# Hybrid decoder trunk on one core: projection pieces paced over all heads, a reciprocal in quarters, weight splits in halves

## The chip, the cores and the metric

One core of a Trainium2 chip runs the kernel as one program. The metric is the device time of one execution in microseconds. Before the change three executions took 1368.0, 1368.33 and 1369.17 us; the median is 1368.33 us.

## What is computed

Two layers, 512 positions of width 1024, all in fp32:

```python
h = rms_norm(x, attn_pre_norm[l])
proj = h @ w_in[l]                       # 1024 x 2844: q, k, v of three head groups
o_fox = fox_attention(...)               # 4 heads, causal, with a forget gate
o_nsa = nsa_attention(...)               # 8 heads, 2 key groups; compressed + selected + window branches
o_dil = dilated_attention(...)           # 4 heads
x = x + rms_norm(concatenate([o_fox, o_nsa, o_dil]) @ w_out[l], attn_post_norm[l])
h = rms_norm(x, ffn_pre_norm[l])
x = x + rms_norm((silu(a) * b) @ w_down[l], ffn_post_norm[l])   # a, b = causal conv(h @ w_up[l])
```

The compressed branch of the nsa heads makes its keys and values by `gelu(win @ w1) @ w2` over 31 windows of 32 positions.

## The kernel before, in words

**Products in two parts.** A weight arrives by DMA as fp32 (`raw`); `part_weights` (L137) makes a high part `wh` on ScalarE (ACT, L146) and the rest `wl = raw - wh` on VectorE (DVE, L154) or GpSimd (POOL, L150). Activations are split likewise (`hh`, `hl`; `ph`, `pl`; `mix`). Each product is three matmuls: high x high, low x high, high x low. `getw` (L202) issues the load of a weight two places ahead in a fixed plan and its split one or two places ahead. `DCUTS` (L42) lists the weights whose split is made in two instructions per engine instead of one, cut along the second axis (k). The weights `wo2` (rows 4 to 7 of `w_out`, 128x1x1024) have only one k, and are made whole.

**Attention as a list of units.** A unit is one head branch and one block t of 128 queries; 4 fox heads x 4, then 8 nsa heads x 2 branches x 4, then 4 dilated heads x 4 make 96 units (L1079). In slot i of the loop at L1241 the stages of different units run with fixed lags: scores of unit i on TensorE (PE, tile `s`), mask and minimum on DVE (L1126), exponential on ACT (L1131) and reciprocal on DVE (L1139), normalizing on POOL (L1143), transposes on PE five slots later (L1156, tile `pt`, two banks), the split of the transposed block on ACT (`ph`, L1167) and DVE (`pl`, L1172), and products with the values seven slots later (tile `o`). PE's order is the program's order (`tc.manual_schedule`); the other engines' order is set by the scheduler.

**Pieces between the units.** The projections that later heads need, the gelu's hidden layer, and the first half of the output projection are cut into pieces of about 12 matmuls (generator `main_pieces`, L750): 8 x 8 pieces of `proj256`, 2 x 4 of `hidden`, 16 of `out_first` (`wo`), 88 in all. `step()` issues one piece. A budget decides how many pieces follow each slot: it grows by 1.4 a slot in the first 12 slots and by 0.8 after that (`RATE`, L1231); a unit that needs a tensor not yet made forces pieces at once (`until`). After the 88, `out_start` (L918) issues nothing before slot 95; its pieces are the products with `wo2`.

**The gelu chain.** `cmp_pieces` (L938) makes gelu, compressed keys and values and the compressed scores, one step per slot (`chain_step`). One of its steps holds two reciprocals of 128x128 on DVE (L952). `cmp_values` then adds the compressed result to a head pair.

After the loop come the rest of the output projection, the norms, and the feed-forward part, whose first weights are `("up", 0, 0..3)`.

Of the kernel before, what the change touches and what calls it, by code (L numbers as in the profile page):

```python
# [12 lines left out]
AF = mybir.ActivationFunctionType  # L13
# [23 lines left out]
PCUT = ((0, 2), (2, 4))  # L37
# [1 line left out]
TT = "pt"  # L39
CT = "acc"  # L40
FIRST = 5
DCUTS = ("w1", "wo")  # L42
EV = (1, 3, 1, 1)
ORDER = (0, 1, 2, 4, 3, 5, 6, 7, 8)
HA0 = (1, 3)
# [29 lines left out]
def tile_hybrid_block(  # L75
# [6 lines left out]
    nc = tc.nc  # L82
# [12 lines left out]
    def nm(p):  # L95
        uid[0] += 1
        return f"{p}_{uid[0]}"
# [4 lines left out]
    def bt(shape, dt=F32, name="b"):  # L102
        return big.tile(shape, dt, tag="b", name=nm(name))

    def rt(shape=(128, 512), dt=F32):
        return rowp.tile(list(shape), dt, tag="r", name=nm("r"))
# [4 lines left out]
    def f(ap):  # L111
        return ap.bitcast(F32)
# [18 lines left out]
    def load(srcs, nk, ncol, tagn=""):  # L131
        raw = wpool.tile([128, nk, ncol], F32, tag="raw", name=nm("raw" + tagn))
        for s, k0, o in srcs:
            nc.sync.dma_start(raw[:, k0:k0 + s.shape[1], o:o + s.shape[2]], s)
        return raw

    def part_weights(raw, nk, ncol, spare, tagn, pool, cut):  # L137
        DCUT = ((0, 2), (2, 4)) if cut else ((0, 4),)
        if spare:
            hi, lo = bt([128, nk, ncol], F32R, "wh"), bt([128, nk, ncol], F32R, "wl")  # L140
        else:
            hi = wpool.tile([128, nk, ncol], F32R, tag="wh", name=nm("wh" + tagn))
            lo = wpool.tile([128, nk, ncol], F32R, tag="wl", name=nm("wl" + tagn))
        for a, e in HCUT if pool else DCUT:
            ks = slice(nk * a // 4, nk * e // 4)
            nc.scalar.activation(hi[:, ks], raw[:, ks], AF.Copy)  # L146
        if pool:
            for a, e in PCUT:
                ks = slice(nk * a // 4, nk * e // 4)
                nc.gpsimd.tensor_sub(lo[:, ks], raw[:, ks], f(hi)[:, ks])  # L150
        else:
            for a, e in DCUT:
                ks = slice(nk * a // 4, nk * e // 4)
                nc.vector.tensor_sub(lo[:, ks], raw[:, ks], f(hi)[:, ks])  # L154
        return hi, lo

    plan, ready = [], {}
# [2 lines left out]
    def kview(w, l):  # L160
        return w[l].rearrange("(k p) c -> p k c", p=128)

    for l in range(DEPTH):
        wi, wo, wu, wd = (kview(w, l) for w in (w_in, w_out, w_up, w_down))
# [37 lines left out]
    def getw(*key, ahead=AHEAD, pre=None, peek=False):  # L202

        i = where[key]
        pre = ahead if pre is None else min(pre, ahead)
        tag = lambda k: "_".join(str(z) for z in k)
        for n in range(len(done)):
            upto = i + (ahead, pre)[n]
            while done[n] < len(plan) and done[n] <= upto:
                k, srcs, nk, ncol, spare = plan[done[n]]  # L210
                if n == 0:
                    ready[k] = load(srcs, nk, ncol, tag(k))
                else:
                    ready[k] = part_weights(ready[k], nk, ncol, spare, tag(k), k[1] in ONPOOL or k[1:4] in ONPOOL or k[0:3] in ONPOOL,
                                            k[1] in DCUTS)
                done[n] += 1
        return None if peek else ready.pop(key)

# [142 lines left out]
    load_x(0)  # L361
    load_x(1)
    getw(0, "fk", 0, ahead=0, pre=-1, peek=True)
    grow = rt((2 * DEPTH * KT, 128))
    for i, src in enumerate((attn_pre_norm, ffn_pre_norm)):
        nc.sync.dma_start(grow[DEPTH * KT * i:DEPTH * KT * (i + 1), :], src.rearrange("l (k p) -> (l k) p", p=128))
    getw(0, "fk", 0, ahead=1, pre=-1, peek=True)
    load_x(2)
    getw(0, "fk", 0, ahead=2, pre=-1, peek=True)
    load_x(3)  # L370
    wk = []
# [76 lines left out]
    for l in range(DEPTH):  # L448
# [208 lines left out]
        nc.vector.tensor_scalar(gates, gates, 1.0, None, op0=ALU.add)  # L657
        nc.vector.reciprocal(gates, gates)

        mix, sums = {}, {}  # L660
        OFIRST = (0, 1, 2, 3)

        def split_mix(k, eng, cs=slice(0, 512)):
            if k not in mix:
                if k != 7:
                    mix[k] = bt([128, 2, 512], F32R, "mix")
                else:
                    mix[k] = ptp.tile([128, 2, 512], F32R, tag="ph", name=nm("mix"))
            d = mix[k]
            nc.scalar.activation(d[:, 0, cs], sums[k][:, cs], AF.Copy)  # L670
            eng.tensor_sub(d[:, 1, cs], sums[k][:, cs], f(d[:, 0, cs]))

        def o_mms(o, s, ks, w, first, last):

            sl = slice(128 * s, 128 * s + 128)
            for i, k in enumerate(ks):
                hi, lo = w[2 * i][:, 0], w[2 * i + 1][:, 0]
                mm(o, mix[k][:, 0, sl], hi, first and i == 0, False)
                mm(o, mix[k][:, 0, sl], lo, False, False)
                mm(o, mix[k][:, 1, sl], hi, False, last and i == len(ks) - 1)  # L680
# [20 lines left out]
        slot = [0]  # L701
        pieces, chain = Pieces(), []
# [47 lines left out]
        def main_pieces():  # L750
# [87 lines left out]

            for k in OFIRST:
                while k not in mix:  # L840
# [4 lines left out]
            def out_first():  # L845
                for qd in range(4):
# [3 lines left out]
                    for s in range(NST):  # L850
                        o_mms(sl256(pp, s), s, OFIRST, w4, s % 2 == 0, s % 2 == 1)
                        pieces.later(1, lambda s=s, q=sl256(pp, s), qd=qd: nc.scalar.activation(
# [32 lines left out]
        def mid_load(s):  # L885
            xt = bt([128, DM], name="x")
            nc.sync.dma_start(xt, x[0, 128 * s:128 * s + 128, :] if l == 0 else xsv[128 * s:128 * s + 128, :])
            xs.append(xt)
            hs.append(bt([128, DM], name="h"))
# [48 lines left out]
        def cmp_pieces(xc, w2r):  # L938

            t1, t2 = rt((128, 256)), rt((128, 256))  # L940
# [7 lines left out]
            nc.scalar.activation(t2, t1, AF.Exp, scale=-2.0 * math.sqrt(2.0 / math.pi))  # L948
            yield
            nc.vector.tensor_scalar(t2, t2, 1.0, None, op0=ALU.add)  # L950
            for c in range(2):
                nc.vector.reciprocal(t2[:, 128 * c:128 * c + 128], t2[:, 128 * c:128 * c + 128])  # L952
            yield
            nc.gpsimd.tensor_mul(xc, xc, t2)
            yield
            yield
# [105 lines left out]
        def step():  # L1062
            pieces.n += 1
            ended = next(fill, "end") == "end"
            pieces.due(last=ended)
            if ended and not chain:
                live[0] = False

        def chain_step():
            for c in chain:  # L1070
                if next(c, "end") == "end":
                    chain.remove(c)
# [6 lines left out]
        units = []  # L1079
# [132 lines left out]
        def cmp_values(k):  # L1212

            p = ps("pt")
            gq, part = k // 2, slice(64 * (k % 2), 64 * (k % 2) + 64)
            pch, pcl = store["pc"]
            vh, vl = (vcm[part, gq, i].rearrange("p u d -> p (u d)") for i in range(2))
            mm(p, vh, pch[part, gq, :], True, False)
            mm(p, vh, pcl[part, gq, :], False, False)
            mm(p, vl, pch[part, gq, :], False, True)  # L1220
            nc.vector.tensor_add(sums[2 + k], sums[2 + k], p)
            split_mix(2 + k, nc.gpsimd)
# [5 lines left out]
                mm(p[:, sl], hi[:, k, :], HL(k)[:, sl], False, False)  # L1228
                mm(p[:, sl], lo[:, k, :], HH(k)[:, sl], False, last and k == KORDER[-1])

        RATE = [1.4] * 12 + [0.8] * 98  # L1231
        LM, LN, LT, LE, LV, LO = LAGS
        stages = ((0, st_scores), (LE, st_keep_hi), (LM, st_max), (LN, st_norm), (LE, st_keep_lo), (LM, st_exp),
                  (LV, st_values), (LT, st_turn), (LO, st_out))
# [1 line left out]
        budget = 0.0  # L1236
        with tc.manual_schedule(engines={mybir.EngineType.PE}):
            for i in range(FIRST):
                step()
            for i in range(len(units) + LO):  # L1240
                slot[0] = i  # L1241
                U = lambda lag: units[i - lag] if 0 <= i - lag < len(units) else None
                for lag, fn in stages:
                    if U(lag) is not None:
                        fn(U(lag))
                budget += RATE[i]
                while budget >= 1.0:
                    budget -= 1.0
                    if live[0] or pieces.late:
                        step()  # L1250
                chain_step()
                if store.get("pc") and whole and whole[0][1] <= i:
                    cmp_values(whole.pop(0)[0])
            while whole or live[0] or pieces.late:
                if whole and store.get("pc"):
                    cmp_values(whole.pop(0)[0])
                elif live[0] or pieces.late:
                    step()
                    chain_step()
            for s in range(2):  # L1260
                mid_load(s)
            ws = [getw(l, "up", 0, n, ahead=0) for n in range(2)]
# [160 lines left out]
```

## Time and profile before

| what | before |
|---|---|
| median of the runs shown | 1368.33 us |
| the profiled execution's own time | 1369.85 us |
| its span, first to last instruction | 1367.9 us |
| PE busy | 1338.0 us (98%) |
| DVE, ACT, POOL busy | 850.4, 728.2, 287.0 us |
| granted TensorE clock, mean | 0.998 |

A profile's times are from the span's start. Layer 0's attention loop starts at about 62 us and its last unit's scores at 290 us; the feed-forward matmuls run to about 680 us; layer 1 repeats the same from there. A matmul's end is modelled, so a row's duration is its passage through the array, and the pace is read from one start to the next: 0.12 us for 128x256, 0.23 us for 128x512.

### The profile page before, as it was taken

The page shows a single profiled execution, that of the slowest core. Times are in us where ns is not written, and L with a number is a line of the kernel's source. Part 1 is how long each engine was busy: PE and PEld are TensorE (multiplying, and loading weights), DVE is VectorE, ACT ScalarE, POOL GpSimd, SP SyncE. Part 2 cuts the span into 40 slices and gives each one's busy share as a digit, 9 for nine tenths or more (in the row PEclk, how much of TensorE's full clock was granted, in tenths as well). Part 3 has the DMA queues.
Part 4 walks back from the last instruction along what each step waited for, and adds up shares of the span by engine and source line. Part 5 has one row for each costly group of instructions (what it writes and reads, how often), then busy time and mean ns, then how long its engine had stood idle before and what let it go on. Part 6 is the DMA issues. An engine that isn't in the chain of part 4 may idle for free.

```text
span 1367.9 us, 21028 instructions
## 1 busy us (share of the span) xinstructions
PE 1338.0 (98%) x7855; PEld 1177.9 (86%) x7855; DVE 850.4 (62%) x1893; ACT 728.2 (53%) x1506; POOL 287.0 (21%) x343
## 2 busy tenths in 40 slices
PE   9999999999999999999999999999999999999997
PEld 8899998978888888888898999999798888888886
DVE  7677787677755555433464887777876555554334
ACT  6567767777533333333465677667774333333232
POOL 2364753341000000000004647634210000000000
PEclk9999999999999999999999999999999999999999
DMA  6323311131333333333333242111323333332231
GB/s 181 94 63 115 104 35 48 58 128 33 107 93 103 97 92 96 104 93 123 111 96 93 63 139 63 47 41 58 120 62 98 103 92 93 104 97 92 94 122 62
DMA packets 145517, 123.74 MB, mean 90 GB/s; under 512 B 8264, under 2 KB 135688, under 8 KB 145416
## 3 DMA queue, kind: packets, MB, share of 16 engines
q1 hardware_dynamic: 145416, 122.40, 29.5%
q8 instruction: 62, 1.02, 0.3%
q14 instruction: 39, 0.32, 0.1%
HBM read 118.19 MB, written 4.19 MB: 89 GB/s over the span
## 4 chain that ended last, share of the span: by engine, by line
PE 85%; DVE 7%; ACT 4%; POOL 2%; issue 2%; DMA 0%; SPq 0%; ACTq 0%; POOLq 0%; DVEq 0%
PE acc L115 39%; PE s L115 19%; PE pt L115 13%; PE o L115 10%; PE pt L1156 3%; POOL wt L795 1%; PE pt L737 1%; DVE hl L271 1%; DVE pl L1172 1%; DVE r L1126 1%; ACT r L1131 1%; DVE x L913 0%; ACT hh L270 0%; ACT h L310 0%; ACT ph L1167 0%
## 5 line engine op out<-in xcount | busy, mean ns | idle before, releaser
L154 DVE TENSOR_TENSOR wl_up<-raw_up,wh_up 128x1024 fp32r<-128x1024 f32 x78 | 95.6, 1225 | 170.8 <-ACT wh_up L146 170.8
L146 ACT ACTIVATE wh_up<-raw_up 128x1024 fp32r<-128x1024 f32 (+1 forms) x90 | 89.6, 1001 | 160.4 <-PE acc L115 68.1
L154 DVE TENSOR_TENSOR wl_wd<-raw_wd,wh_wd 128x1024 fp32r<-128x1024 f32 x42 | 51.5, 1225 | 133.7 <-ACT wh_wd L146 133.7
L146 ACT ACTIVATE wh_wd<-raw_wd 128x1024 fp32r<-128x1024 f32 x42 | 44.5, 1060 | 144.8 <-PE pt L115 135.5
L1143 POOL TENSOR_SCALAR r<-r,sm,gates 128x128 f32<-128x128 f32 (+3 forms) x128 | 86.4, 683 | 126.1 <-DVE sm L1139 82.3
L1131 ACT ACTIVATE r<-r,sm 128x128 f32<-128x128 f32 x192 | 106.7, 557 | 9.3 <-DVE sm L1126 8.4
L115 PE MATMUL acc<-hh,wl_up 128*128 128x512 f32 (+1 forms) x272 | 102.4, 376 | 0.0
L115 PE MATMUL acc<-hl,wh_up 128*128 128x512 f32 (+1 forms) x272 | 102.4, 376 | 0.0
L115 PE MATMUL acc<-hh,wh_up 128*128 128x512 f32 (+1 forms) x272 | 102.4, 376 | 0.0
L150 POOL TENSOR_TENSOR wl_kc<-raw_kc,wh_kc 128x512 fp32r<-128x512 f32 x8 | 11.8, 1490 | 417.6 <-ACT wh_kc L146 416.8
L115 PE MATMUL s<-k,q 128*128 128x512 f32 (+3 forms) x384 | 96.2, 337 | 0.6 <-DVE sm L1126 0.6
L1172 DVE TENSOR_TENSOR pl<-pt,ph 128x384 fp32r<-128x384 f32 x144 | 85.6, 596 | 17.3 <-ACT ph L1167 15.9
L1167 ACT ACTIVATE ph<-pt 128x384 fp32r<-128x384 f32 x144 | 75.4, 523 | 29.1 <-PE pt L1156 27.9
L1126 DVE CUSTOM_DVE_ANT_0 r<-s,cmask 128x128 f32<-128x128 f32 (+3 forms) x160 | 76.0, 482 | 20.6 <-PE s L115 16.2
L1156 PE MATMUL pt<-ident,r 128*128 128x128 f32 x480 | 77.5, 276 | 7.0 <-DVE pl L1172 5.5
L115 PE MATMUL acc<-wh_wd,gh 128*128 128x512 f32 x252 | 83.7, 389 | 0.0
L115 PE MATMUL s<-hh,wh_up 128*128 128x512 f32 (+1 forms) x224 | 80.4, 359 | 0.0
L115 PE MATMUL s<-hl,wh_up 128*128 128x512 f32 (+1 forms) x224 | 80.4, 359 | 0.0
L115 PE MATMUL s<-hh,wl_up 128*128 128x512 f32 (+1 forms) x224 | 80.4, 359 | 0.0
L1347 ACT ACTIVATE r<-r 128x512 f32<-128x512 f32 x44 | 27.8, 632 | 85.7 <-DVE r L1328 85.5
L1156 PEld LDWEIGHTS pt<-ident,r 128*128 128x128 f32 x480 | 55.4, 141 | 15.9 <-POOL r L1143 6.8
L115 PE MATMUL acc<-wh_wo,mix 128*128 128x256 f32 (+1 forms) x296 | 67.6, 305 | 0.0
(439 smaller groups left out, 4121.2 us busy)
## 6 DMA issues: line engine op xcount, KB each, us to landing
raw_up<-in_w_up_dram SPq DMA_DIRECT2D x88, 512.0 KB, 3.8
raw_wd<-in_w_down_dram SPq DMA_DIRECT2D x44, 512.0 KB, 3.4
raw_wo<-in_w_out_dram SPq DMA_DIRECT2D x16, 512.0 KB, 3.5
x<-in_x_dram SPq DMA_DIRECT2D x8, 512.0 KB, 5.9
raw_nq<-in_w_in_dram SPq DMA_DIRECT2D x8, 512.0 KB, 3.7
raw_w<-in_cmp_w_k_dram SPq DMA_DIRECT2D x8, 512.0 KB, 4.0
raw_w<-in_cmp_w_v_dram SPq DMA_DIRECT2D x8, 512.0 KB, 4.2
raw_fk<-in_w_in_dram SPq DMA_DIRECT2D x4, 512.0 KB, 5.9
```

The source lines that it names most:

```text
L115: nc.tensor.matmul(o, lhsT=lhsT, rhs=rhs, start=start, stop=stop, skip_group_check=True)
L146: nc.scalar.activation(hi[:, ks], raw[:, ks], AF.Copy)
L154: nc.vector.tensor_sub(lo[:, ks], raw[:, ks], f(hi)[:, ks])
L271: nc.vector.scalar_tensor_tensor(lo, src, gain[:, k:k + 1], f(hi), op0=ALU.mult, op1=ALU.subtract)
L737: nc.tensor.transpose(p[:, 128 * s:128 * s + 128], tl[s][:, 128 * j:128 * j + 128], ident)
L1126: nc.vector.tensor_tensor_reduce(row[:, 0:n], u["S"][:, 0:n], u["mask"][:, 512 - n:512], op0=ALU.add, op1=ALU.min, scale=1.0, scalar=3.0e3 ...
L1131: nc.scalar.activation(row[:, 0:n], row[:, 0:n], AF.Exp, scale=-1.0, bias=sm_[0], accum_out=sm_[1])
L1143: nc.gpsimd.tensor_scalar(row[:, 0:n], row[:, 0:n], z["sm"][2], g_, op0=ALU.mult, op1=ALU.mult)
L1156: nc.tensor.transpose(p[:, 128 * c:128 * c + 128], blocks[z], ident)
L1167: nc.scalar.activation(hi, src, AF.Copy)
L1172: nc.vector.tensor_sub(*u["lo"])
L1347: nc.scalar.activation(cd[0], cd[0], AF.Silu)
```

## The change

1. **Pace.** The fixed 0.8 pieces a slot become `(88 - pieces.n) / (slots left)`, counted anew in each slot, so that the 88 pieces end with the last unit.
2. **Reciprocal.** The two 128x128 reciprocals of the gelu chain become four of 128x64, each a chain step of its own; the chain's later steps come three slots later.
3. **Weights in halves.** `wo2` and `("up", 0, 0)` are added to the weights that are split in two instructions per engine; a weight with a single k is cut by columns.

`OLAG` and `kept` are set and never read.

```diff
-DCUTS = ("w1", "wo")
+DCUTS = ("w1", "wo", "wo2")
...
+        def cutting(z, a, e):
+            return z[:, nk * a // 4:nk * e // 4] if nk > 1 else z[:, :, ncol * a // 4:ncol * e // 4]
+
         for a, e in HCUT if pool else DCUT:
-            ks = slice(nk * a // 4, nk * e // 4)
-            nc.scalar.activation(hi[:, ks], raw[:, ks], AF.Copy)
-        if pool:
-            for a, e in PCUT:
-                ks = slice(nk * a // 4, nk * e // 4)
-                nc.gpsimd.tensor_sub(lo[:, ks], raw[:, ks], f(hi)[:, ks])
-        else:
-            for a, e in DCUT:
-                ks = slice(nk * a // 4, nk * e // 4)
-                nc.vector.tensor_sub(lo[:, ks], raw[:, ks], f(hi)[:, ks])
+            nc.scalar.activation(cutting(hi, a, e), cutting(raw, a, e), AF.Copy)
+        for a, e in PCUT if pool else DCUT:
+            (nc.gpsimd if pool else nc.vector).tensor_sub(cutting(lo, a, e), cutting(raw, a, e), cutting(f(hi), a, e))
...
-                                            k[1] in DCUTS)
+                                            k[1] in DCUTS or k[1:3] == ("up", 0))
...
-            for c in range(2):
-                nc.vector.reciprocal(t2[:, 128 * c:128 * c + 128], t2[:, 128 * c:128 * c + 128])
-            yield
+            for c in range(4):
+                nc.vector.reciprocal(t2[:, 64 * c:64 * c + 64], t2[:, 64 * c:64 * c + 64])
+                yield
...
-        RATE = [1.4] * 12 + [0.8] * 98
+        NPIECES = 8 * 8 + 2 * 4 + 16
...
-                budget += RATE[i]
+                budget += 1.4 if i < 12 else max(NPIECES - pieces.n, 0.8) / max(len(units) - i, 1)
```

How the order moves, at three places of layer 0. On PE, around the scores of the second dilated head (slots 84 to 86; `s<-k,q` are scores, `pt<-ident,r` transposes, `acc<-wh_wo,mix` a piece of the output projection). Before:

```order
L1156 MATMUL pt_4064<-ident,r_3992 128x128 x4
L115 MATMUL s_4069<-k_3612,q_3204 128x128 x2
L115 MATMUL s_4069<-k_3612,q_3204 128x256 x2
L1156 MATMUL pt_4090<-ident,r_4015 128x128
L1156 MATMUL pt_4090<-ident,r_4032 128x128 x2
L115 MATMUL s_4094<-k_3612,q_3204 128x384 x2
```

and with the change (the first three of a piece's 12 matmuls are shown each time):

```order
L1154 MATMUL pt_3943<-ident,r_3856 128x128 x4
L115 MATMUL s_3948<-k_3783,q_3351 128x128 x2
L115 MATMUL acc_3960<-wh_wo_753_3759,mix_1483 128x256
L115 MATMUL acc_3960<-wl_wo_754_3760,mix_1483 128x256
L115 MATMUL acc_3960<-wh_wo_753_3759,mix_1483 128x256
...
L115 MATMUL s_3948<-k_3783,q_3351 128x256 x2
L1154 MATMUL pt_3992<-ident,r_3866 128x128
L1154 MATMUL pt_3992<-ident,r_3899 128x128 x2
L115 MATMUL acc_3960<-wh_wo_753_3759,mix_1483 128x256
...
L115 MATMUL s_4009<-k_3783,q_3351 128x384 x2
```

Where scores and transposes followed each other directly, a piece of 12 matmuls now stands in most slots.

On DVE, around the gelu chain's reciprocals (slots 33 to 37 before; `ISA` is the mask and minimum L1126, `q` a projection's split). Before:

```order
L950 TENSOR_SCALAR r_2303<-r_2303 128x256
L1126 ISA r_2395,sm_2397<-s_2342,cmask 128x384
L1126 ISA sm_2397 128x1
L952 RECIPROCAL r_2303<-r_2303 128x128 x2
L1139 RECIPROCAL sm_2310<-sm_2310 128x2
L490 SCALAR_TENSOR_TENSOR q_2421<-pt_2378,q_2421 64x512
L1126 ISA r_2431,sm_2433<-s_2391,cmask 128x512
L1126 ISA sm_2433 128x1
L1172 TENSOR_TENSOR pl_2346<-pt_2404,ph_2345 128x512
```

and with the change (three of the four quarters; the fourth follows six rows below):

```order
L950 RECIPROCAL r_2340<-r_2340 128x64
L1124 ISA r_2400,sm_2402<-s_2384,cmask 128x128
L1124 ISA sm_2402 128x1
L1137 RECIPROCAL sm_2389<-sm_2389 128x1
L950 RECIPROCAL r_2340<-r_2340 128x64
L1124 ISA r_2440,sm_2441<-s_2384,cmask 128x256
L1124 ISA sm_2441 128x1
L1170 TENSOR_TENSOR pl_2438<-pt_2407,ph_2437 128x384
L486 SCALAR_TENSOR_TENSOR q_2472<-pt_2423,q_2472 64x512
L950 RECIPROCAL r_2340<-r_2340 128x64
L1204 TENSOR_TENSOR mx_2203<-o_2301,r_2457 64x512
L486 SCALAR_TENSOR_TENSOR q_2472<-pt_2423,q_2472 64x512
```

The attention's own work now stands between the parts of the reciprocal.

On DVE, at the end of the attention loop (`wl_4295`, with the change `wl_4307`, is the low part of `wo2` row block 5). Before:

```order
L1172 TENSOR_TENSOR pl_4246<-pt_4262,ph_4245 128x384
L1126 ISA r_4307,sm_4309<-s_4272,dmask 128x512
L1126 ISA sm_4309 128x1
L1139 RECIPROCAL sm_4277<-sm_4277 128x1
L154 TENSOR_TENSOR wl_4295<-raw_wo_5_767_3898,wh_4294 128x1024
L1172 TENSOR_TENSOR pl_4246<-pt_4285,ph_4245 128x512
```

and with the change:

```order
L1137 RECIPROCAL sm_4267<-sm_4267 128x1
L1170 TENSOR_TENSOR pl_4236<-pt_4275,ph_4235 128x512
L150 TENSOR_TENSOR wl_4307<-raw_wo_5_839_4142,wh_4306 128x512
L1137 RECIPROCAL sm_4295<-sm_4295 128x1
L150 TENSOR_TENSOR wl_4307<-raw_wo_5_839_4142,wh_4306 128x512
L1170 TENSOR_TENSOR pl_4336<-pt_4323,ph_4335 128x384
```

The last block of the third dilated head's `pl` stood behind the weight's split and stands ahead of its first half now.

## Rows read from the trace of the kernel before

**Rows 1.** Part 1 of the page: busy time of each engine, share of the span, instructions.
```profile
PE 1338.0 (98%) x7855; PEld 1177.9 (86%) x7855; DVE 850.4 (62%) x1893; ACT 728.2 (53%) x1506; POOL 287.0 (21%) x343
```

**Rows 2.** Busy time by stretch: window, its length, then busy us (instructions) of PE, PEld, DVE, ACT, POOL, the granted clock, DMA share, GB/s. Fox and nsa heads to slot 33 or so; the gelu's reciprocals (160 to 168); nsa heads; dilated heads and the loop's end (272 to 297); rest of the output projection and norms; feed-forward. Then layer 1's reciprocals, nsa heads and dilated heads.
```profile
62.00:160.00 98.00, 97.42 (x773) 94.54 (x773) 72.09 (x220) 69.66 (x186) 58.08 (x62) 1.00 0.32 93
160.00:168.00 8.00, 6.18 (x50) 5.63 (x49) 7.50 (x22) 6.03 (x17) 5.53 (x8) 1.00 0.31 83
168.00:272.00 104.00, 101.85 (x788) 96.63 (x788) 77.90 (x244) 71.74 (x190) 47.30 (x65) 1.00 0.15 47
272.00:297.00 25.00, 21.93 (x141) 18.49 (x140) 20.62 (x65) 22.53 (x59) 15.11 (x21) 1.00 0.24 70
297.00:340.00 43.00, 41.77 (x269) 37.28 (x268) 32.82 (x79) 29.01 (x65) 5.51 (x4) 1.00 0.29 95
340.00:680.00 340.00, 340.00 (x1530) 282.53 (x1529) 173.76 (x208) 127.49 (x166) 0.00 (x0) 1.00 0.34 101
834.00:843.00 9.00, 7.17 (x58) 6.63 (x57) 8.14 (x22) 7.02 (x19) 6.53 (x9) 1.00 0.20 58
843.00:946.00 103.00, 100.82 (x768) 95.62 (x766) 75.64 (x240) 70.37 (x187) 45.21 (x65) 0.98 0.15 47
946.00:973.00 27.00, 23.94 (x157) 20.49 (x156) 22.61 (x68) 23.48 (x60) 16.48 (x22) 1.00 0.22 65
```

**Rows 3.** Timeline of PE in the dilated heads, with the idle time before a row and what ended it.
```profile
277.63 0.52 PE L1156 MATMUL pt<-ident,r 128*128 128x128 f32 x3 [0.57 <-DVE pl L1172]
...
281.81 0.50 PE L115 MATMUL pt<-pch,vcm 64*128 64x512 f32 x1 [0.80 <-DVE pl L1172]
282.16 0.39 PE L115 MATMUL pt<-pcl,vcm 64*128 64x512 f32 x1
...
287.69 0.52 PE L1156 MATMUL pt<-ident,r 128*128 128x128 f32 x3 [0.65 <-DVE pl L1172]
...
294.28 0.40 PE L115 MATMUL o<-ph,v 128*128 128x512 f32 x1
295.74 0.50 PE L115 MATMUL o<-pl,v 128*128 128x512 f32 x1 [1.06 <-DVE pl L1172]
```

**Rows 4.** Timeline of DVE just before that last wait.
```profile
292.92 0.16 DVE L1139 RECIPROCAL sm<-sm 128x1 f32<-128x1 f32 x1
293.60 1.48 DVE L154 TENSOR_TENSOR wl<-raw_wo,wh 128x1024 fp32r<-128x1024 f32 x1 [0.52 <-ACT wh L146]
295.00 0.68 DVE L1172 TENSOR_TENSOR pl<-pt,ph 128x512 fp32r<-128x512 f32 x1
```

**Rows 5.** Timeline around the gelu's reciprocals: PE's two waits, and DVE.
```profile
161.70 0.73 PE L115 MATMUL s<-k,q 128*128 128x512 f32 x2 [0.31 <-DVE sm L1126]
...
166.27 0.52 PE L1156 MATMUL pt<-ident,r 128*128 128x128 f32 x3 [1.52 <-DVE pl L1172]
...
162.29 1.76 DVE L952 RECIPROCAL r<-r 128x128 f32<-128x128 f32 x2
163.97 0.11 DVE L1139 RECIPROCAL sm<-sm 128x2 f32<-128x2 f32 x1
164.11 0.69 DVE L490 SCALAR_TENSOR_TENSOR q<-pt,q 64x512 fp32r<-64x512 f32 x1
164.82 0.69 DVE L1126 CUSTOM_DVE_ANT_0 r<-s,cmask 128x512 f32<-128x512 f32 x1
165.44 0.69 DVE L1172 TENSOR_TENSOR pl<-pt,ph 128x512 fp32r<-128x512 f32 x1
```

**Rows 6.** PE's waits between 168 and 272 us (who waited for whom: us in total, times, longest). In this stretch lie eight slots without a piece, each alone between slots that have one.
```profile
PE acc L1039 <- DVE pcl L1047: 0.7, 1, 0.7
PE pt L1156 <- DVE mx L1221: 0.5, 1, 0.5
PE pt L737 <- DVE pl L1172: 0.5, 1, 0.5
PE pt L1156 <- DVE k L497: 0.2, 1, 0.2
PE pt L115 <- DVE q L490: 0.2, 1, 0.2
```

**Rows 7.** Instructions by line and tile: count, min/median/max ns, first and last start, shapes.
```profile
L952 DVE RECIPROCAL r<-r x4: 894/922/948, 162.3 to 837.8; 128x128 f32<-128x128 f32 x4
L1139 DVE RECIPROCAL sm<-sm x144: 101/162/168, 67.1 to 971.7; 128x1 f32<-128x1 f32 x96, 128x2 f32<-128x2 f32 x48
L154 DVE TENSOR_TENSOR wl_wo<-raw_wo,wh_wo x20: 672/687/1226, 207.7 to 941.6; 128x512 fp32r<-128x512 f32 x16, 128x1024 fp32r<-128x1024 f32 x4
L146 ACT ACTIVATE wh_wo<-raw_wo x20: 614/619/1065, 203.8 to 940.5; 128x512 fp32r<-128x512 f32 x16, 128x1024 fp32r<-128x1024 f32 x4
```

**Rows 8.** Busy time and granted clock (columns as in rows 2) where layer 1's nsa heads wait, and two rows of PE's timeline there.
```profile
890.00:895.00 5.00, 3.83 (x22) 2.81 (x21) 4.45 (x11) 3.21 (x8) 0.97 (x2) 0.90 0.10 30
895.00:900.00 5.00, 5.00 (x32) 4.91 (x31) 2.01 (x4) 2.59 (x8) 2.08 (x3) 0.76 0.21 79
...
895.30 0.41 PE L115 MATMUL acc<-wh_dk,hl 128*128 128x256 f32 x1
895.51 0.41 PE L115 MATMUL acc<-wh_dk,hh 128*128 128x256 f32 x1
```

More of the change, by code (lines that the diff above doesn't have):

```diff
@@ L658, in tile_hybrid_block @@
         nc.vector.reciprocal(gates, gates)
-        mix, sums = {}, {}
+        mix, sums, kept = {}, {}, {}
         OFIRST = (0, 1, 2, 3)
+        OLAG = 200
         def split_mix(k, eng, cs=slice(0, 512)):
@@ L669, in split_mix @@
             d = mix[k]
+            kept[k] = slot[0]
             nc.scalar.activation(d[:, 0, cs], sums[k][:, cs], AF.Copy)
```

## The prediction

> **What bounds the kernel now.** First the page's busy times: PE is busy in 98% of the span, DVE in 62% [rows 1]. Matmul rows overlap, so that alone says little; what is to be read is where PE still waits. The busy times by stretch show it: the feed-forward stretch of 340 us has 340.00 us of PE, and fox and early nsa heads 97.42 of 98 [rows 2]. The idle time lies in the attention loop: 25.00 - 21.93 = 3.07 us in layer 0's dilated heads and the loop's end, 8.00 - 6.18 = 1.82 us in the few slots around the gelu's reciprocals, 104.00 - 101.85 = 2.15 us in the remaining nsa heads. Layer 1 has 3.06, 1.83 and 2.18 us in the same places [rows 2]. Every one of these waits names DVE as its releaser [rows 3, 5, 6]. So the end is set by PE's program order, and a change helps by the PE idle time it removes, one for one; PE's matmuls are the same in number and shape before and after.
>
> **The pace.** Before, 40 of the 88 pieces are issued by slot 20 (forced ones among them), and 0.8 a slot use up the other 48 by slot 80. From slot 81 to 94 there is no piece: 14 slots in a row in which PE has a unit's scores, transposes and value products alone. There PE waits four times for `pl`: 0.57, 0.80, 0.65 and 1.06 us, 3.08 us in all [rows 3], the same 3.07 us as by stretch, at a DVE busy in 20.62 of 25 us [rows 2]. After each wait the first row takes 0.50 instead of 0.39 or 0.40 us [rows 3]; I add 0.1 us a wait, so the run costs 3.5 us a layer. Now (88 - 40) / 76 = 0.63 pieces a slot reach slot 95, and no two slots without a piece follow each other. A piece of 12 matmuls of 128x256 is 12 x 0.12 = 1.44 us of PE work, which covers the longest of these waits.
>
> What is paid for it: slots 20 to 80 get fewer pieces. Slots without a piece were 11 lone ones and the run of 14; they are 27 lone ones. The price of a lone one is to be read between 168 and 272 us, where eight stand. PE's five waits there sum to 2.1 us [rows 6]; two of them (0.2 for `k`, 0.5 for `mx`) come in or right behind a slot without a piece, so a lone slot costs between 0.2 / 8 = 0.03 and 0.7 / 8 = 0.09 us. I take 0.06, since the 0.5 us one stands behind `cmp_values`, which is there anyway. The upper end, however unlikely, is the mean of the run: 3.07 / 14 = 0.22 us. Sixteen more lone slots cost 16 x 0.06 = 1.0 us a layer (0.5 to 3.5). Net gain of the pace: 3.5 - 1.0 = 2.5 us a layer.
>
> **The reciprocals.** Two of 0.92 us [rows 7] stand together on DVE from 162.29, 1.76 us; behind them come 0.11, 0.69 and 0.69 us and then the `pl` for which PE stands from before 166.27, 1.52 us [rows 5]. With quarters, one stands ahead of any `pl`, not four. A quarter is not in the trace: half of 0.92 is 0.46 us, and the smallest reciprocal, of one column, takes 0.16 us [rows 7], which bounds the fixed part, so 0.46 to 0.54 us; I take 0.5. Three quarters less in front are 1.5 us, about the whole wait. But the 8 us have 7.50 us of DVE work [rows 2], so some of it will stand elsewhere: I count 1.3 us a layer, between 0.7 (half given back) and 1.9 (both waits and their refill). The 0.31 us wait at 161.70 lies ahead of the reciprocals and stays. The chain's three later steps cost nothing: `mix` 2 and 3, which the output pieces need first, come some 13 slots before the first of them. DVE has strictly more work, 2 x 0.08 us at most for the reciprocals.
>
> **Weights in halves.** Five weights a layer become ten instructions on each of ACT and DVE. Two halves take 2 x 0.69 against 1.23 us on DVE and 2 x 0.62 against 1.06 us on ACT [rows 7]: 5 x 0.15 = 0.75 us and 5 x 0.18 = 0.9 us more, on engines with 4 us and more to spare in the stretch that now gets longer. The last of the four waits, 1.06 us, is a `pl` behind a `wl` of 1.48 us on DVE [rows 4]; in the new order that `pl` is ahead of the first half. I don't count it twice: it is in the 3.5 us. `("up", 0, 0)` is wanted some 20 us later: nothing.
>
> [...]
>
> **Sum.** A layer gains 2.5 + 1.3 = 3.8 us, both layers 7.6 us. The profiled execution took 1369.85 us, 1.5 above the median; it would take 1362.2, and the median of 1368.33 becomes **1360.7 us**. The best of the bounds: 3.5 - 0.5 + 1.9 = 4.9 a layer, 9.8, with the clock's dip (below) gone 11.5 us: 1356.8. The worst: 3.5 - 3.5 + 0.7 a layer, 1.4 us: 1366.9.
>
> **Rivals.** *Given back.* DVE, not the order, sets the pace of the nsa heads: it is busy 77.90 of 104 us there [rows 2], and with less PE work a slot its share rises. If each lone slot costs 0.22 us as in the run, the pace gains nothing, and what the quarters spare is spent in the same backlog: 1367 to 1368 us. Against it: seven of the eight lone slots brought no wait of a unit's own [rows 6]. Chance 0.13.
>
> [...] Chance 0.07.
>
> *The pace does not reach the end,* because steps that issue nothing also count as pieces. The order printed shows pieces between the dilated scores, so 0.02 at most; its time would be the quarters' alone, 1365.7 us.
>
> **How the numbers follow.** About 0.2% (2.7 us) is what a measurement of this kernel can tell from no change, so faster means under 1365.6 us. The forecast has 0.78, a small part of it above that line. The range goes from 1356.0, the best of the bounds with some room, to 1367.4, into the first rival; the slower one is left out. Faster 0.77, within 0.2% 0.16, slower 0.07.
>
> **What would show it.** Right: the stretch of the dilated heads is some 10 us longer, with PE waits under 0.5 us instead of 3.07; four reciprocals of about 0.5 us apart from each other, and no PE wait over 0.5 us near them; two `wl` of 0.69 us for each `wo2`. Wrong: PE waits in the nsa heads that sum to more than 3 us above the 2.15 of now, or a granted clock under 0.95 in several stretches, or the longest wait moved to the loop's end, where `wo2` is wanted.

## The result, and the profile after

The changed kernel took 1377.31 us (median of 6 runs, 1375.96 to 1378.25), the kernel before 1368.75 us beside it: ratio 1.0058, 95% interval 1.0046 to 1.0070. That is 8.6 us slower, outside the range given and with the other sign. The profiled execution's span went from 1367.9 to 1375.3 us, and PE's matmuls are the same in number (answers to [rows 1]):

```profile
PE 1340.0 (97%) x7855; PEld 1179.9 (86%) x7855; DVE 856.0 (62%) x1907; ACT 730.3 (53%) x1516; POOL 283.4 (21%) x343
```

Layer 0 by stretch after the change, columns as in [rows 2]: the reciprocals, the nsa heads up to the compressed scores, those scores with their transposes, the later nsa heads, the dilated heads; last the compressed scores of layer 1.

```profile
158.00:170.00 12.00, 10.26 (x77) 9.14 (x76) 9.40 (x24) 9.11 (x22) 6.67 (x11) 1.00 0.34 95
170.00:186.00 16.00, 15.46 (x122) 14.64 (x123) 11.20 (x41) 11.66 (x36) 10.75 (x15) 1.00 0.10 34
186.00:214.00 28.00, 23.64 (x179) 22.54 (x179) 22.11 (x74) 15.51 (x41) 15.68 (x24) 0.94 0.12 39
214.00:265.00 51.00, 49.33 (x369) 45.99 (x368) 40.63 (x125) 37.10 (x98) 19.00 (x27) 1.00 0.13 42
265.00:299.00 34.00, 33.25 (x246) 31.07 (x245) 25.88 (x73) 27.61 (x75) 13.19 (x20) 1.00 0.20 63
...
864.00:893.00 29.00, 24.63 (x187) 23.54 (x186) 22.42 (x75) 15.94 (x43) 16.55 (x25) 0.94 0.12 38
```

The dilated heads did what was forecast: 0.75 us of PE idle in 34 us, where [rows 2] had 3.07 in 25. Around the reciprocals PE idles as long as before, 1.74 us in 12, where [rows 2] had 1.82 in 8. And 4.36 us are idle between 186 and 214 us, at a granted clock of 0.94. The same part of the chain before (slots 42 to 50, compressed scores and transposes) stood at:

```profile
177.00:205.00 28.00, 27.34 (x217) 26.33 (x216) 23.06 (x84) 16.87 (x48) 18.54 (x27) 1.00 0.13 39
```

PE's timeline of the changed kernel shows where: `acc<-ident,r` are the chain's transposes (`c_turn`, L1037) of query blocks 0 and 1. `acc` is one of the program's sets of PSUM banks, into which its products go; it has three.

```profile
201.06 0.38 PE L1037 MATMUL acc<-ident,r 128*128 128x128 f32 x2
...
205.74 0.66 PE L1037 MATMUL acc<-ident,r 128*128 128x128 f32 x2 [3.73 <-DVE pcl L1045]
...
206.84 0.63 PE L115 MATMUL o<-ph,v 128*128 128x512 f32 x1
207.26 0.63 PE L115 MATMUL o<-pl,v 128*128 128x512 f32 x1
```

Block 1's transposes waited 3.73 us for `pcl` of block 0, the last reader of an `acc` bank; then a 128x512 took 0.42 us from start to start, not 0.23, at a granted clock of 0.50 (206 to 208 us). Why `pcl` was late is read from DVE's timeline, then POOL's:

```profile
201.65 0.95 DVE L1030 TENSOR_TENSOR sm<-sm,gates 128x8 f32<-128x8 f32 x1
204.63 0.42 DVE L1027 TENSOR_REDUCE sm<-r 128x8 f32<-128x256 f32 x1 [2.02 <-POOL r L1026]
...
205.17 0.42 DVE L1045 TENSOR_TENSOR pcl<-acc,pch 128x256 fp32r<-128x256 f32 x1
...
201.31 1.27 POOL L150 TENSOR_TENSOR wl_dk<-raw_dk,wh_dk 128x512 fp32r<-128x512 f32 x1
202.57 0.77 POOL L1141 TENSOR_SCALAR r<-r,sm,gates 128x512 f32<-128x512 f32 x1
203.30 0.61 POOL L1031 TENSOR_TENSOR r<-r,sm 128x256 f32<-128x256 f32 x1
203.87 0.72 POOL L1026 TENSOR_TENSOR r<-r,cvalid 128x256 f32<-128x256 f32 x1
```

DVE's queue stood 2.02 us at the sum of block 3 (L1027), which waited for POOL; POOL had three other instructions first; `pcl` of block 0 stood behind that sum. PE's two longest groups of waits between 168 and 272 us, where [rows 6] had 0.7 and 0.5:

```profile
PE acc L1037 <- DVE pcl L1045: 4.4, 2, 3.7
PE pt L1154 <- DVE k L493: 1.2, 1, 1.2
```

The quarters and the halves took (answers to [rows 7]; count, min/median/max ns; the second row is two of the four `wo2` weights of each layer):

```profile
L950 DVE RECIPROCAL r<-r x8: 532/544/554, 164.9 to 849.8; 128x64 f32<-128x64 f32 x8
...
L150 DVE TENSOR_TENSOR wl<-raw_wo,wh x8: 675/925/1375, 282.8 to 976.7; 128x512 fp32r<-128x512 f32 x8
```

### The profile page after: what moved, and what is told of

The parts are those of the page before. It is cut to its first block, busy times and chain, and to the rows that moved or that the text cites. A ratio compares the mean times of both kernels' runs of the same rounds, so it can differ in the third digit from the quotient of the medians.

```text
span 1375.3 us, 21039 instructions
## 1 busy us (share of the span) xinstructions
PE 1340.0 (97%) x7855; PEld 1179.9 (86%) x7855; DVE 856.0 (62%) x1907; ACT 730.3 (53%) x1516; POOL 283.4 (21%) x343
## 4 chain that ended last, share of the span: by engine, by line
PE 82%; DVE 7%; POOL 4%; ACT 4%; issue 2%; DMA 1%; SPq 0%; POOLq 0%; ACTq 0%; DVEq 0%
PE acc L115 37%; PE s L115 18%; PE pt L115 12%; PE o L115 10%; PE pt L1154 3%; POOL wt L793 1%; PE pt L735 1%; DVE hl L267 1%; POOL r L1141 1%; POOL wl_dq L150 1%; DVE r L1124 1%; POOL wl_dv L150 0%; DVE pl L1170 0%; ACT hh L266 0%; DVE x L911 0%
## 5 line engine op out<-in xcount | busy, mean ns | idle before, releaser
L1141 POOL TENSOR_SCALAR r<-r,sm,gates 128x128 f32<-128x128 f32 (+3 forms) x128 | 82.4, 652 | 114.3 <-DVE sm L1137 72.1
```

Source lines behind the costliest of these rows:

```text
L1141: nc.gpsimd.tensor_scalar(row[:, 0:n], row[:, 0:n], z["sm"][2], g_, op0=ALU.mult, op1=ALU.mult)
```

## The experiments

"Before" ran beside each at 1367.9 to 1368.1 us. Differences below are between medians.

| kernel | us | ratio to before (95%) |
|---|---|---|
| e1 pace alone | 1370.49 | 1.0014 (1.0005 to 1.0023) |
| e2 quarters alone | 1383.56 | 1.0107 (1.0093 to 1.0121) |
| e3 halves alone | 1368.33 | 0.9999 (0.9990 to 1.0007) |
| e10 delay of 3 slots alone | 1384.09 | 1.0113 (1.0100 to 1.0126) |
| e11 quarters, chain's place kept | 1368.46 | 0.9998 (0.9989 to 1.0006) |
| e12 chain 3 slots earlier | 1380.18 | 1.0087 (1.0074 to 1.0100) |
| e14 delay of 9 slots | 1380.54 | 1.0099 (1.0083 to 1.0114) |
| e5 changed, transposes a slot later | 1382.22 | 1.0095 (1.0081 to 1.0108) |
| e13 changed, shared bank | 1377.58 | 1.0069 (1.0056 to 1.0082) |
| e18 changed, one bank a projection | 1371.08 | 1.0021 (1.0013 to 1.0030) |
| e19 quarters, one bank a projection | 1378.20 | 1.0067 (1.0055 to 1.0080) |
| e21 changed, transposes in `s` | 1380.61 | 1.0086 (1.0072 to 1.0099) |
| e22 changed, dk split on DVE | 1377.88 | 1.0074 (1.0061 to 1.0086) |
| e25 changed, ACT frees the bank | 1378.07 | 1.0059 (1.0045 to 1.0073) |
| e15 pace, split at once | 1366.75 | 0.9986 (0.9977 to 0.9995) |
| e23 changed, one bank, split at once | 1368.28 | 1.0002 (0.9993 to 1.0011) |
| e24 pace, one bank, split at once | 1367.90 | 0.9996 (0.9987 to 1.0005) |
| e26 pace, split at once, ACT frees | 1371.49 | 1.0021 (1.0012 to 1.0030) |

**The parts alone (e1, e2, e3).** Each is the kernel before with the lines of one part of the diff.

> The kernel before with the new pace alone (one reciprocal step, weights whole). Theory M, a meeting of parts: the loss is the two long waits of the chain's transposes (3.9 us in layer 0, some 5 in layer 1, with the slow clock behind them), and these need the chain's last steps both late by five slots and behind a POOL weight split. With the pace alone they are late by two slots, and the order puts two of the wl_dk splits ahead of the chain's second step: no wait over 1 us at the chain's transposes, dilated heads gain 3.5 a layer, empty slots cost 1.0: about 1364. Theory P, the pace itself: with a piece in 6 of 10 slots instead of 8 the nsa heads have too little beside the units, whatever the chain does: slower than before, 1374 to 1378. Theory Q, the three slots alone: the pace is the gain, 1362 to 1364.

> The kernel before with the reciprocal in four quarters, one a step, alone. Theory M: the chain comes three slots later, but the slots around its transposes keep their pieces and the wl_dk splits stand ahead of the chain: the wait of 1.5 us at the reciprocals goes, about 1366. Theory P: the same, 1366. Theory Q: the three slots of delay make the loss, the chain's transposes wait 3 us or more in each layer here too: 1373 or more.

> The kernel before with the weights in halves alone (wo2 and the first up weight). Theories M, P and Q: within 1 us of before, 1368 to 1370. If the halves carry the loss, by a split placed ahead of something that PE waits for: 1372 or more.

The first theory, a meeting of pace and delay, fell: the quarters alone lose 15.5 us, more than the whole change. The halves are nothing. The pace gains nothing either: it loses 2.4 us, between what theories M and P gave.

**What of the quarters costs (e10, e11, e12, e14).** e10 and e14 put 3 or 9 idle steps behind the two old half reciprocals; e11 and e12 drop three idle steps, with quarters and without:

```diff
 # e10 (e14: range(9))
             yield
+            for _ in range(3):
+                yield
 # e11, e12: the yield between the reciprocals and tensor_mul is dropped, and
             nc.gpsimd.tensor_mul(xc, xc, t2)
-            yield
             yield
...
                 nc.vector.tensor_sub(hvl[:, j], src, f(hvh[:, j]))
-            yield
             yield
```

> The kernel before, its two half reciprocals in one step as they were, with three idle steps behind them. Theory S, the chain's place: the delay alone carries the loss, since it puts the compressed scores and their transposes (eight acc tiles, one a slot) where the dq and dk projections each hold two of the three acc banks: 1383 to 1386, the quarters' own gain missing. Theory R, the quarters themselves (smaller DVE instructions, another order on DVE): 1367 to 1370, as before.

> The kernel before with the reciprocal in four quarters, one a step, and three idle steps of the chain left out behind them, so that the compressed scores stand in the slots of before (42 to 45). Theory S: no loss, and the wait of 1.5 us at the reciprocals goes in each layer: 1365 to 1367. Theory R: the loss of the quarters alone stays, 1380 to 1385.

> The kernel before, reciprocals as they were, with the same three idle steps left out: the chain comes three slots earlier than before. Theory S: no fixed price per slot of lateness; the scores fall at the end of dv (its two banks go without a rotary stage), the transposes into dq as before: 1364 to 1370. If lateness as such costs (5 us a slot over both layers, as from the quarters alone): 1355 or less.

> The kernel before with nine idle steps behind the reciprocals, so that the compressed scores come at slots 51 to 54 and the transposes at 56 to 59. If each slot of lateness has a price (5 us a slot from three slots): 1400 or more. If the price is one of meeting dq's rotary stage and the dk splits at slots 45 to 53: less than the three slots cost, 1370 to 1380.

The delay is the loss: without quarters it costs 16.0 us, and quarters without delay cost nothing. It is no price per slot: nine slots cost 12.5 us, less than three, and three slots earlier cost 12.1, where theory S had forecast at most 2. PE's waits in the quarters-alone kernel, 184 to 216 us:

```profile
PE acc L115 <- DVE acc L473: 1.9, 1, 1.9
PE acc L115 <- DVE r L1018: 1.5, 1, 1.5
PE s L115 <- DVE sm L1126: 1.1, 1, 1.1
PE acc L1039 <- DVE r L476: 0.8, 1, 0.8
```

Three of four are for an `acc` bank. The second is for the second read of the chain's block before (L1018). The first and the last bear the names of the dq projection's rotary stage (L473, L476), but the times say otherwise. In the twenty traces PE has 565 waits over 0.15 us with a DVE instruction's name. In 546 it starts 0.05 to 0.06 or 0.14 to 0.15 us after that instruction's end. In the other 19, these two among them, it starts 0.00 to 0.07 us after it, and each time DVE's last read of the chain's tile before had ended 0.15 us ahead of PE's start. So these too are waits for the chain's own bank. DVE's timeline shows why that read (L1017, L1018) was late, for the 1.94 us wait:

```profile
198.32 0.23 DVE L471 TENSOR_TENSOR rope<-acc,ss 128x64 f32<-128x64 f32 x1 [2.41 <-PE acc L115]
...
198.99 0.41 DVE L1017 TENSOR_TENSOR r<-acc,cinv 128x256 f32<-128x256 f32 x1
...
199.67 0.41 DVE L1018 TENSOR_TENSOR r<-r,acc 128x256 f32<-128x256 f32 x1
200.00 0.23 DVE L473 TENSOR_TENSOR acc<-acc,cc 128x64 f32<-128x64 f32 x1
```

```profile
200.23 1.05 PE L115 MATMUL acc<-kcm,q 128*128 128x64 f32 x8 [1.94 <-DVE acc L473]
```

DVE's queue had the rotary stage ahead of the chain's read and stood 2.41 us for dq's piece on PE. The program says why one bank matters so: `proj256` (L702 of the changed kernel) opens two of the three `acc` banks and uses both until its eight pieces are evacuated, so the chain's eight tiles, one a slot, go through the third. With the scores three slots earlier PE waits elsewhere too (160 to 200 us): the first of these rows is, by its times, again for the chain's tile before (`pcl`), the others are for the gelu's own results:

```profile
PE acc L1036 <- DVE sm L1029: 1.2, 1, 1.2
PE acc L115 <- DVE r L968: 1.2, 1, 1.2
PE acc L115 <- DVE kcm L990: 1.1, 1, 1.1
```

and nine slots later for the last copies of dq's rotary stage (ACT, L477) and the chain's own tiles (190 to 240 us):

```profile
PE acc L115 <- ACT r L477: 2.5, 2, 1.6
...
PE acc L1041 <- DVE r L1020: 1.2, 1, 1.2
PE acc L1041 <- DVE pcl L1049: 1.0, 1, 1.0
PE acc L115 <- DVE r L1020: 1.0, 1, 1.0
```

**What the transposes wait for (e5, e13, e18, e19, e21, e22, e25).** Short forms of the edits, all on the changed kernel but e19, which is e2 with the second edit:

```diff
 # e5
-CL = (1, 3, 5, 6)
+CL = (1, 3, 6, 7)
 # e18, e19, in proj256, for dq and dk: blocks 0 and 1 over both weight chunks, then 2 and 3
-            for c in range(2):
+            for c, half in ((0, 0), (1, 0), (0, 1), (1, 1)):
...
-                for s in range(NST):
+                for s in (2 * half, 2 * half + 1):
 # e13, in c_turn: a new tile for every second block only, which takes the other half
+                if t % 2 == 0:
+                    rows["p"] = ps(CT)
+                p = rows["p"][:, 256 * (t % 2):256 * (t % 2) + 256]
 # e21, in c_turn
-                p = ps(CT)
+                p = ps("s")
 # e22
-ONPOOL = ("dv", "dq", "dk", ...
+ONPOOL = ("dv", "dq", ...
 # e25, in c_keep
+                copy = rt((128, 2, 128))
+                nc.scalar.activation(copy, src, AF.Copy)
-                nc.scalar.activation(pch[:, :, sl], src, AF.Copy)
-                nc.vector.tensor_sub(pcl[:, :, sl], src, f(pch[:, :, sl]))
+                nc.scalar.activation(pch[:, :, sl], copy, AF.Copy)
+                nc.vector.tensor_sub(pcl[:, :, sl], copy, f(pch[:, :, sl]))
```

> The changed kernel with the chain's transposes (c_turn) and the keeping of their result one slot later after the normalizing: CL = (1, 3, 6, 7) for (1, 3, 5, 6). Theory M: the transposes no longer come before POOL and DVE are done with the block ahead; the wait of 3.9 us in layer 0 falls to under 1.5, the one in layer 1 likewise: 1377 minus 5 to 9, about 1370. Theory P: the waits come from thin slots and move with the chain, no change, 1375 to 1378. Theory Q: one slot later is one more delay, 1377 to 1380.

> The changed kernel with the chain's transposes of two query blocks in the two halves of one acc tile, so that the second block's transposes need no bank back. Theory S: the wait of 3.7 us before the second block's transposes in layer 0 goes, and with it most of the two waits in layer 1 that stand there; a wait before the third block's may take a part of it: 1367 to 1372. If the transposes wait for their own input rows instead of the bank: 1375 to 1378, no change.

> The changed kernel with the dq and dk projections' pieces in another order (query blocks 0 and 1 over both weight chunks, then 2 and 3), so that each holds one acc bank and then the other, in place of both for eight pieces. Theory S2 (the delayed chain's tiles go through the one acc bank that is left while PE waits in order for DVE to read it): the wait of 3.7 us at the chain's transposes falls to under 1 in each layer, and no half clock follows: 1377 minus 8 to 11, 1366 to 1369. Theory D (DVE and POOL are late with the chain's rows whatever the banks): 1375 to 1378.

> The kernel before with the quarters (chain three slots later) and the same order of the dq and dk pieces. Theory S2: most of the 15 us of the delay goes, since the waits of 1.5 and 1.9 us before the compressed scores and the 0.8 before the transposes are for banks: 1368 to 1374. Theory D: 1381 to 1385.

> The changed kernel with the chain's transposes in the banks of the scores (tag s) in place of acc. Theory S2: the 3.7 us wait for an acc bank goes, some new waits of the units' scores for their banks come: 1368 to 1374. Theory D: the scores' tile is now held as long as acc was and PE waits there: 1375 to 1380.

> The changed kernel with the split of the dk weights (wl_dk, four times 1.27 us on POOL in each layer) made on DVE. Theory G (DVE's queue stands 2.0 us at a reduction of the chain that waits for POOL, and POOL has wl_dk ahead of the row it needs): the wait of 3.7 us in each layer falls to under 1.5 and the half clock with it, while DVE has 2.7 us more work a layer: 1377 minus 4 to 9, 1368 to 1373. If POOL's queue is not what makes the row late: 1376 to 1382.

> The changed kernel with the chain's transposed rows copied whole by ACT to SBUF first (four more ACT copies of 128x256, 0.4 us each, a layer); both parts are made from the copy, so that the acc bank is free when ACT is done and no longer when DVE is. Theory G2 (PE waits 3.7 us because the bank's last reader, pcl on DVE, stands in DVE's queue behind a reduction of a later query block that waits for POOL): the wait falls to under 1.5 in each layer and the half clock behind it goes: 1377 minus 6 to 10, 1367 to 1371. If the transposes were held up by their own rows or by ACT: 1375 to 1379.

One bank a projection (e18) takes 6.2 us off the changed kernel (5.3 if each is compared with the kernel before beside it) and 5.4 off the quarters alone (e19), less than theory S2 gave. That share belongs to the edit, which frees the banks and also moves DVE's and POOL's instructions; no run separates the two. In the changed kernel the 3.73 us became two shorter waits of PE:

```profile
201.36 0.41 PE L1040 MATMUL acc<-ident,r 128*128 128x128 f32 x2 [0.55 <-DVE rope L467]
...
203.58 0.61 PE L1040 MATMUL acc<-ident,r 128*128 128x128 f32 x2 [1.24 <-issue]
```

The first is for the chain's tile before, by its times another of the 19 (L1019); before the second PE starts 0.10 us after ACT's copy for the rotary stage (L473). One of the two stretches at the lower clock is gone: the mean granted clock of the profiled execution is 0.998, the changed kernel's 0.996.

Where the wait went in e19, and in the edits that gained nothing, PE's timelines show. In order: one bank a projection with the quarters alone, transposes in `s`, dk split on DVE, ACT frees.

```profile
206.55 0.69 PE L115 MATMUL s<-k,q 128*128 128x128 f32 x2 [3.85 <-DVE sm L1129]
```

```profile
205.53 0.41 PE L1037 MATMUL s<-ident,r 128*128 128x128 f32 x2 [3.74 <-DVE pcl L1045]
```

```profile
205.68 0.41 PE L1037 MATMUL acc<-ident,r 128*128 128x128 f32 x2 [3.56 <-DVE sm L1028]
```

```profile
201.93 0.41 PE L1037 MATMUL acc<-ident,r 128*128 128x128 f32 x2 [0.21 <-ACT r L1045]
...
208.06 0.50 PE L1037 MATMUL acc<-ident,r 128*128 128x128 f32 x2 [2.38 <-POOL r L1143]
```

In e19 the long wait went from `acc` to a unit's scores. In e25 it went from block 1 to block 2: PE starts there 0.10 us after ACT's copy of block 1, which stood in ACT's queue behind an exponential that had waited 2.71 us for DVE:

```profile
205.01 0.40 ACT L1131 ACTIVATE r<-r,sm 128x128 f32<-128x128 f32 x1 [2.71 <-DVE sm L1126]
...
207.59 0.38 ACT L1045 ACTIVATE r<-acc 128x256 f32<-128x256 f32 x1
```

In e22 PE's wait is still for `pcl` (0.15 us before its start; the name in the row is another of the 19). DVE makes the `dk` split itself and stands at the same sum until the same time; beside that split a product of POOL took 1.46 us in place of 0.61, so e22 does not show that the split is harmless. Its DVE timeline, then POOL's:

```profile
202.16 1.21 DVE L150 TENSOR_TENSOR wl_dk<-raw_dk,wh_dk 128x1024 fp32r<-128x1024 f32 x1
204.57 0.42 DVE L1027 TENSOR_REDUCE sm<-r 128x8 f32<-128x256 f32 x1 [1.19 <-POOL r L1026]
```

```profile
202.39 1.46 POOL L1031 TENSOR_TENSOR r<-r,sm 128x256 f32<-128x256 f32 x1 [0.16 <-DVE sm L1030]
```

So the wait does not follow one bank or the engine that frees it. What the traces have in common is DVE's stop at the chain's sum, waiting for POOL: 2.0 us in each layer of the changed kernel, of e5, e13, e21 and e25, 1.2 us in e22, and none over 0.3 us in the kernel before and in e18, the one edit of this group that gained on the changed kernel. It is not all: e19 gained on the quarters alone with stops of 2.2 and 1.2 us, where those have one of 1.2. My reading is that DVE and POOL hand each block of rows to and fro in queues that kept their order (ACT had ended the high part of block 0 at 202.07 us; DVE made its `pcl` at 205.17, behind the sum at 204.63), and PE stops at whichever tile they owe it next; no edit changed that order alone. e13 settles nothing: block 1's transposes still wait for DVE's reading of block 0's half of the bank (8.8 us in total, 8.7 without the edit). e5 split the wait at the transposes (2.4 and 1.6 us in layer 0, before the edit 3.73 and 0.63) and added one of 1.2 us for `mx`; its loss of 4.9 us to the changed kernel refutes my first theory's forecast of a gain.

**Why the pace gains nothing (e15, e23, e24, e26).** e15 is e1 with:

```diff
+                empty = budget < 1.0 and i >= 24
+                for z in [z for z in pieces.late if empty and z[2].__name__ == "keep"]:
+                    pieces.late.remove(z)
+                    z[2](*z[3])
```

`keep` splits a turned block and frees its `pt` bank; without the edit it waits for the next piece. e23 is the changed kernel with this and e18's edit, e24 is e15 with e18's, e26 is e15 with e25's.

> The kernel before with the pace alone, but in a slot without a piece a turned projection block (tile pt) is split at once by ACT and DVE instead of after the next piece. Theory K (the pace alone gives its gain back because a piece-less slot leaves a turned block in one of the two pt banks, which the units' transposes then wait for, 1.3 and 1.2 us in each layer): these waits go, 1370.5 minus 3 to 5, 1366 to 1368. If the gain is given back elsewhere: 1369 to 1372.

> The changed kernel with one acc bank at a time for dq and dk, and turned blocks split at once in slots without a piece. If the two causes add: 1371.1 minus 3.7, 1366 to 1368.5. If the at-once split gains only where the chain is not late: 1370 to 1372.

> The kernel before with the pace, the at-once split, and one acc bank at a time for dq and dk (chain as in before, no quarters, weights whole). Theory S2: the waits of 1.05 and 0.5 us at the chain's transposes that the pace alone has go too: 1363 to 1366. If the projection's new order costs as much: 1366.5 to 1368.

> The kernel before with the pace, turned blocks split at once in slots without a piece, and the same freeing of the bank by ACT (no quarters, weights whole). Theory G2: the waits of 1.05 and 0.5 us at the chain's transposes in each layer go too: 1366.75 minus 1 to 3, 1363.5 to 1366. If DVE or ACT is then late elsewhere: 1366.5 to 1368.

e15 gains 3.7 us on e1 and is the only kernel faster than before, by 0.14%. Of the waits of pace alone (130 to 300 us),

```profile
PE pt L737 <- DVE q L490: 1.3, 1, 1.3
PE pt L1156 <- DVE k L497: 1.2, 1, 1.2
PE pt L1156 <- DVE pl L1172: 1.0, 2, 0.8
```

the one for `k` is gone in e15 and that for `pl` is 0.2, while the ones for `q` grow from 1.3 and 0.3 to:

```profile
PE pt L1156 <- DVE q L490: 1.4, 1, 1.4
PE pt L737 <- DVE q L490: 1.0, 1, 1.0
```

In the changed kernel the two edits add: 6.2 and then 2.8 us, back to the time of before (e23). On e15 the bank edits do not help (e24 +1.2, e26 +4.7 us), against the forecast of 1 to 3 us of gain: perhaps there was less to gain with the chain at its old distance, and in e26 PE waits for `pch` behind the extra copies, 3.8 us in both layers.

## Why the prediction was wrong, point by point

- **The failed step** is "the chain's three later steps cost nothing". I looked only for who needs the chain's end (`mix`), and not at what its steps hold on the way: an `acc` bank a slot, and places in DVE's and POOL's queues. Measured alone, the step costs 15.5 to 16.0 us.
- *The size in the changed kernel.* In the nine slots from the first compressed scores to the last transposes I summed, from one start to the next, what each PE row took above its undisturbed pace. Before: 3.3 us a layer in 25.9 us. After: 8.3 and 8.5 us in 25.7 us, since those slots hold 17.3 us of PE work instead of 22.6 (four without a piece instead of one) and still last as long. Quarters alone: 10.2 and 9.3 us in 30.1 and 29.2 us. So the loss there is 5.0 and 5.1 us, 10.1 in both layers, against 8.6 in the result.
- *Pace, the gain.* Right in place and near in size: the dilated stretch is longer and its four waits are gone. 0.75 us are left, one wait for `part` at its end, so the idle time fell by 2.3 us; with the 0.4 us for the rows after the waits that is 2.7 of the 3.5.
- *Pace, the price.* Mis-sized: 16 more lone slots were put at 1.0 us a layer (3.5 at most). Pace alone lost 2.4 us, so with a gain of 2.7 to 3.5 us they cost 3.9 to 4.7 us a layer. I had divided the waits by eight slots of which only one held a turned block; e15 shows some 1.9 us a layer of it to be `pt` banks held over a slot without a piece; where the rest lies no run shows.
- *The quarters.* A quarter takes 0.54 us, the upper end of what I gave; four of them are 0.33 us more DVE work than two halves, where I had put 0.16 at most (2 x 0.08; by the 0.54 it is 4 x 0.08). With the chain's place kept, PE's wait there was 0.8 us instead of 1.52, for `q`, and the median did not change measurably; 1.3 us a layer was too much. e11's executions go from 1366.95 us at a mean clock of 0.999 to 1370.09 at 0.996, so the clock may have taken back a part. In the changed kernel the wait of 1.52 us for `pl` is gone, but one of 1.3 us for `q`, which the pace alone has too, ends as the first quarter starts, against the sign of no wait over 0.5 us near them.
- *The halves.* Right: nothing. In half of the `wo2` weights a half took 0.93 us at the median, not 0.69, still hidden.
- *Rivals.* Slower was right, at chance 0.07 a result I had all but left out. With the pace alone PE waits 1.2 us for `k`, a turned block held over an empty slot, but the granted clock stayed at 1.00 in the loop (mean of the profiled execution 0.999). The lower clock came with the chain's waits: in the changed kernel it was granted from 205.0 us on (0.51, then 0.50), in the wait that ended at 205.74. The 11.5 us in the best of the bounds are 9.8 and 1.7 us for the clock's dip, an estimate from [rows 8]: 5 x (1 - 0.90) + 5 x (1 - 0.76); the changed kernel has such a dip in each layer. Two of the signs of "wrong" showed: PE's idle time in the nsa heads (170 to 265 us) sums to 6.6 us, 4.4 above the 2.15 of before, and the granted clock was 0.94 in a stretch of each layer.
- *What stays open.* The parts do not add (15.5 + 2.4 would be 17.9, the whole is 8.6 with the halves), and no run shows why the pace softens the delay. The edit of the banks gives back 5 to 6 us of the changed kernel's 8.6; whether by the banks or by the order that it gives DVE and POOL is open. That the chain's waits come from the to and fro of these two is read from timelines, and no edit removed it alone.

## What to carry to other kernels

A step that is moved in a hand-laid order has to be costed by what it holds where it lands (banks, queue places) as well as by who waits for its end; here a chain lost 12 us by coming three slots earlier and 16 by coming three later. Give a split that needs idle steps the steps from the chain's own slack, as in e11. A pace counted in pieces also delays everything that is due "a piece later", so look for what frees a bank that way before thinning the pieces.

## What the runs showed of the hardware

An estimate, one minus the granted clock summed over its windows, puts a stretch at the lower clock (0.50 granted) at about 1.7 us in three kernels: the kernel before has one, in layer 1 [rows 8], the changed kernel one in each layer, the quarters alone three in all. e1, e11 and e15 have none before the program's end (mean granted clock of the profiled execution 0.999 in each). Longer stretches lost 3.4 us (e12, layer 0) and 5.1 us (e25, layer 1). After the wait at 205.74 us of the changed kernel (columns as in [rows 2]):

```profile
204.00:206.00 2.00, 0.26 (x2) 0.29 (x3) 1.37 (x6) 0.49 (x2) 1.82 (x2) 0.75 0.00 0
206.00:208.00 2.00, 2.00 (x7) 1.81 (x6) 1.39 (x7) 0.87 (x3) 1.01 (x2) 0.50 0.44 137
208.00:210.00 2.00, 2.00 (x17) 2.00 (x17) 0.39 (x1) 0.98 (x2) 0.59 (x2) 0.89 0.41 137
```

The granted clock was 1.00 up to 205.0 us and 0.51 in the half microsecond behind it, so 0.7 us of the lower clock passed while PE still stood. An estimate from these rows: the wait of 3.7 us cost some 5.1, the other 1.3 by the clock.

A DVE product of 128x8 (L1030) took 0.95 us in each layer where the others of its line take 0.15 to 0.26: it began at 201.65 beside POOL's `wl_dk` (201.31, 1.27 us) and ended 0.02 us after it. The kernel before has the same (0.98 us, at 191.54). There POOL's `wl_dk` ran from 191.20 us for 1.29 us, and the product ended 0.03 us after it. That the split held the product up is my reading of these times; no run shows the cause.
